# A two-layer streaming encoder: the modulation tiles of the time mixing start in the fourth period in place of the third

## The chip, the cores and the metric

The kernel runs on one core of one Trainium2 chip, in one launch. The metric is the device time of that launch in microseconds (us), a median over several runs. The core has five engines with a queue each: TensorE (PE, matmuls, with its weight loads PEld), VectorE (DVE), ScalarE (ACT), GpSimd (POOL) and SyncE (SP), which here issues nearly all DMAs.

## The reference

Two layers on 256 tokens of width 2048, 32 heads of 64. Layer 0 is RWKV-7 time mixing and an MLP with squared ReLU (hidden width 8192); layer 1 is a chunked band attention and such an MLP. Each sub-layer's input is normed, shifted and scaled, and its output gated, by vectors computed from a conditioning vector c:

```
mod = c @ w_ada[layer] + b_ada[layer]            # 2048 -> 6 * 2048, in each layer
sh1, sc1, gt1, sh2, sc2, gt2 = jnp.split(mod, 6, axis=-1)
...
h = modulate(rms_norm(x, g_mix[layer]), sh1, sc1)
...
x = x + gt1[:, None, :] * y                       # y: time mixing or attention
h = modulate(rms_norm(x, g_mlp[layer]), sh2, sc2)
x = x + gt2[:, None, :] * sq_relu_mlp(h, w_up[layer], w_down[layer])
```

The shared keys and values of layer 1 have a shift and a scale of their own (w_ada_kv). The time mixing is, per head, a recurrence over tokens; everything is float32.

## The kernel before

**Matmuls.** Weights come as float32 tiles of 128 x 1024 (512 KB, tag `raw`, 6 buffers), two for a block of 128 output columns. `halves` (L371 to L382) splits each into a rounded part `wH` (ACT, L378) and a remainder `wL` (DVE, L381), with 3 buffers each; the activations are split in the same way. `proj2` (L406 to L414) then multiplies a block: per 128 inputs one matmul of `wH` with both parts of the activations (L412) and one of `wL` with the larger part (L413), into a PSUM bank `pj`.

**Modulation.** c is a vector, so c @ w_ada isn't given to PE (but for the first shift and scale, which stand ahead of the time mixing). It is cut into 384 tiles of 128 x 1024 (`ada_tiles`, L427): 12 vectors, two halves each, 16 tiles to a half. `ada_load` (L434) issues a tile's DMA on SP. `ada_step` (L443) takes one tile: one DVE instruction that scales it with its 128 entries of c and adds it to `acc` (L452 for the first of a half, L454 for the others). `acc` has one buffer. When a half has its 16 tiles, `ada_sum` (L471 to L481) adds over the partitions with 32 small matmuls (L476) and one DVE instruction (L480) that writes the vector's half; the next half's first tile waits for the sum. The order of the vectors is fixed: (0, 2), (0, 4), (0, 3), (0, 5), then ("kv", 1), ("kv", 0), and those of layer 1. The pair is the layer and the index in mod above, counted from 0.

Who takes tiles, and how many: `self.ada(n)` takes n. In the time mixing a tile's DMA is issued at the place where it is taken and uses the `raw` buffers. Later, inside `ada_room(n)`, tiles have n buffers of their own (`rada`), and `ada_fill` keeps n - 1 of them loaded ahead. `ada_need(keys)` takes tiles until the named vectors are complete, all at that place.

**The time mixing** (`layer_a`, L630 to L900). The 32 heads are 16 pairs. For each pair the projections k and r are computed (`proj_steps`, 32 steps of one 128-input piece, each two matmuls), and then `Pair.steps`, 36 steps: 8 early ones, 12 that invert a triangular matrix, 16 late ones with the state. An invert step is a short chain through engines: a DVE transpose (`tt`, L239), small matmuls (`iv`, L111), a copy on ACT (L243), matmuls again, an addition on DVE (L254). The slots are a schedule by hand: a loop over 164 slots, 8 to a period (`S = self.SLOTS`), where pair j projects in period j (counted from 0) and makes its 36 steps in the 36 slots after that. So the first period has projections alone, the second adds the early steps of pair 0, the third its first 8 invert steps and pair 1's early steps, and from the sixth on four to five pairs are in work. In each slot every live pair makes one step, then 4 pieces of the projection follow (after slot 127 pieces of the output projection w_o), and then, in three slots of four, one modulation tile is taken.

The order on each engine isn't quite the order in the program: the compiler framework that builds the queues places instructions by their place in the program and by the time at which it expects their inputs and buffers. An instruction can so stand in its engine's queue ahead of others that come earlier in the program, and each queue is then executed in order.

**After the time mixing** `run` demands (0, 2), (0, 4) and (0, 3), 96 tiles, ahead of the output projection. The first MLP (`mlp`, L944 to L1012) has five `rada` buffers. Hidden columns go in four quarters of 16 blocks, each with 16 blocks up and 16 blocks down. `ada_tick` takes 1 and 2 tiles in turn after each block, in the first quarter from the seventh block up on. When the first quarter's 16 blocks up are through, one line demands the gate that the down blocks apply to x (L998):

```
if q == 0:
    self.ada_need((layer, 5))
```

Of the kernel before, what the change touches and what calls it, by code (L numbers as in the profile page):

```python
# [329 lines left out]
class Body:  # L330
# [299 lines left out]
    def layer_a(self, st, sp):  # L630
# [184 lines left out]
        with ExitStack() as s1:  # L815
# [12 lines left out]
            def proj_steps(pr):  # L828
                for dst, hl in (("k", xk), ("r", xr)):
                    w = self.wnext  # L830
                    src = next(weights, None)
                    self.wnext = None if src is None else self.weight(src)
                    ps = pp.tile([P, 2, T], F32, tag="pj", bufs=2, name="pj")
                    for kt in range(KT):
                        self.proj2(ps, w, lambda kt: hl[:, kt, :, 0:T], (kt, kt + 1))
                        if dst == "r" and kt == 1:
                            pr.lw = pw.tile([96, 2, P], F32, tag="lw", bufs=1, name="lw")
                            nc.sync.dma_start(out=pr.lw, in_=d["lora2"][pr.j, :96, 0:2])
                        if kt % 2 == 1:
                            if kt == KT - 1:  # L840
                                t = pw.tile([P, T], F32, tag=dst, bufs=2, name=dst)
                                nc.scalar.copy(t, ps[:, 0, :])
                                nc.vector.tensor_tensor(out=t, in0=ps[:, 1, :], in1=t, op=ALU.add)
                                setattr(pr, dst, t)
                            yield

            def out_steps():

                for n in range(8):
                    self.split(self.y_hl, n, v[:, n, :])  # L850
                sums, todo = self.o_ps, [(n, 0, HK) for n in range(8)] + [(n, HK, KT - 2) for n in range(4)]
                for n, lo, hi in todo:
                    if n % 2 == 0 and lo == 0:
                        tag = ("pj", "pj", "gr", "iv")[n // 2]
                        ps = pp.tile([P, 2 * T], F32, tag=tag, bufs=1 + (tag == "pj"), name="o")
                        sums.append(ps.rearrange("p (i t) -> p i t", i=2))
                    if lo == HK and n == 0:
                        assert all(p.done for p in pairs[:KT - 2])
                        for j in range(HK, KT - 2):
                            self.split(self.y_hl, j, v[:, j, :])  # L860
                    w = self.weight_part(d["w_o"][n], lo, hi)
                    for kt in range(lo, hi, 2):
                        self.proj(sums[n // 2][:, n % 2, :], w, lambda kt: self.y_hl[:, kt, :, 0:T],
                                  (kt, kt + 2), n % 2 == 0, False)
                        yield

            self.o_ps = []
            S, OUTS = self.SLOTS, 44
            inverts = range(Pair.EARLY, Pair.EARLY + Pair.INVERT)
            outs, done, n_out = None, 0, 0  # L870
            for slot in range(S * NPAIR + Pair.STEPS):
                live = []
                for j, pr in enumerate(pairs):
                    at = slot - S * (j + 1)
                    if 0 <= at < Pair.STEPS:
                        if at == 0:
                            pr.gen = pr.steps()
                        live.append((0 if at in inverts else 1 + (at < Pair.EARLY), -at, pr))
                        pr.done = at == Pair.STEPS - 1
                last = self.last_pe()  # L880
                for _, _, pr in sorted(live, key=lambda x: x[:2]):
                    with tc.issue_after(last):
                        next(pr.gen)
                    last = self.last_pe()
                if slot < S * NPAIR:
                    if slot % S == 0:
                        dense = proj_steps(pairs[slot // S])
                    todo = 16 // S
                else:
                    if outs is None:  # L890
                        self.y_hl = self.new_hl()
                        outs = dense = out_steps()
                    todo = OUTS * (slot + 1 - S * NPAIR) // Pair.STEPS - n_out
                    n_out += todo
                with tc.issue_after(last):
                    for _ in range(todo):
                        next(dense, None)
                if slot >= 2 * S and slot % 4 < 3:
                    self.ada()
            self.fin(HK)  # L900
        return v
# [305 lines left out]
```

## Time and profile before

| | |
|---|---|
| median of 3 runs | 2673.67 us (2671.55 to 2675.52) |
| profiled execution, its own time | 2673.81 us |
| its span | 2672.0 us, 1.8 us less than its time |
| granted TensorE clock, mean | 0.994 |
| DMA | 662.64 MB, mean 248 GB/s |
| tiles taken in the time mixing | 111 (first load at 223.8 us, last at 700.2 us) |
| tiles with `rada` buffers | 273 |

Times in the views are us from the start of the span. A group's row gives line, engine, operation, tiles written and read, shape and count. "L111" is line 111 of the kernel. "<-" after an idle time names what ended it. The granted clock is a share of full speed. The time mixing's first projection matmul starts at 209.0 us, the first output block that has all its inputs at 735.5 us, the first MLP runs from 786.5 us, the attention from 1518.2 us and the second MLP from 1938.9 us.

### The profile page before, as it was taken

How to read it: one execution, taken by the hardware profiler on the slowest of the kernel's cores; microseconds unless marked ns; L12 is line 12 of the kernel's file. 1: busy time of each engine (PE TensorE's matmuls, PEld its weight loads, DVE VectorE, ACT ScalarE, POOL GpSimd, SP SyncE). 2: the span in 40 equal slices, each digit the busy share in tenths (PEclk: the TensorE clock that was granted, in tenths of full speed). 3: DMA queues.
4: the chain of work that ended last, by engine and by line, in shares of the span. 5: the costliest groups of instructions: out<-in, count | busy, mean ns of one | idle time of the engine just before them, and what ended most of it. 6: DMA issues, size and time to landing. Idle time of an engine off the chain costs nothing. (4 is left out here: it accounts for less than half of the span.)

```text
span 2672.0 us, 58365 instructions
## 1 busy us (share of the span) xinstructions
PE 2600.1 (97%) x23690; PEld 2225.4 (83%) x23690; DVE 2101.0 (79%) x3109; ACT 1343.9 (50%) x2432; POOL 209.7 (8%) x320
## 2 busy tenths in 40 slices
PE   6999999999999999999999999999999999999997
PEld 3777788788899888888888998877898888888886
DVE  5778888889789888888888898899887556555555
ACT  3345555555456445355365554565564463453554
POOL 0001322332110000000000100000100000000002
PEclk9999999999999999999999999999999999999999
DMA  9966556565768888899898679887766555555553
GB/s 337 314 236 211 192 173 210 189 206 195 245 240 304 324 309 321 322 324 331 320 328 294 238 240 325 324 274 259 264 216 237 186 187 188 189 186 185 189 189 119
DMA packets 217390, 662.64 MB, mean 248 GB/s; under 512 B 21408, under 2 KB 68896, under 8 KB 217120
## 3 DMA queue, kind: packets, MB, share of 16 engines
q1 hardware_dynamic: 215056, 656.36, 71.1%
q8 instruction: 186, 3.05, 0.5%
q10 hardware_dynamic: 2064, 2.54, 0.3%
q14 instruction: 84, 0.69, 0.1%
HBM read 656.72 MB, written 2.10 MB: 247 GB/s over the span
## 5 line engine op out<-in xcount | busy, mean ns | idle before, releaser
L381 DVE TENSOR_TENSOR wL<-raw,wH 128x1024 fp32r<-128x1024 f32 x772 | 940.9, 1220 | 342.6 <-ACT wH L378 337.8
L378 ACT CAST wH<-raw 128x1024 fp32r<-128x1024 f32 x772 | 805.5, 1045 | 801.2 <-PE pj L412 646.0
L412 PE MATMUL pj<-aHL,wH 128*128 128x512 f32 x3328 | 1201.9, 403 | 2.0 <-DVE x L927 1.1
L413 PE MATMUL pj<-aHL,wL 128*128 128x256 f32 x3328 | 936.3, 281 | 0.0
L412 PEld LDWEIGHTS pj<-aHL,wH 128*128 128x128 f32 x3328 | 629.5, 189 | 154.1 <-issue 9.2
L412 PE MATMUL pj<-hHL,wH 128*128 128x512 f32 x2048 | 724.6, 399 | 0.0
L413 PEld LDWEIGHTS pj<-aHL,wL 128*128 128x128 f32 x3328 | 629.7, 189 | 2.6 <-issue 0.8
L413 PE MATMUL pj<-hHL,wL 128*128 128x256 f32 x2048 | 574.7, 281 | 0.0
L412 PEld LDWEIGHTS pj<-hHL,wH 128*128 128x128 f32 x2048 | 384.8, 188 | 95.7 <-DVE hHL L973 0.2
L413 PEld LDWEIGHTS pj<-hHL,wL 128*128 128x128 f32 x2048 | 387.0, 189 | 0.1
L454 DVE SCALAR_TENSOR_TENSOR acc<-rada,ct,acc 128x1024 f32<-128x1024 f32 x256 | 327.5, 1279 | 8.4 <-DMA rada<-w_ada 7.5
L518 POOL TENSOR_TENSOR ss<-ss,sq 128x256 f32<-128x256 f32 x56 | 54.5, 974 | 1590.8 <-ACT sq L517 1590.5
L998 DVE SCALAR_TENSOR_TENSOR x<-pj,mod,x 128x256 f32<-128x256 f32 x256 | 123.3, 482 | 59.5 <-PE pj L413 55.7
L454 DVE SCALAR_TENSOR_TENSOR acc<-raw,ct,acc 128x1024 f32<-128x1024 f32 x104 | 136.4, 1312 | 15.5 <-DMA raw<-w_ada 15.4
L401 PE MATMUL pj<-aHL,wH 128*128 128x258 f32 x384 | 109.0, 284 | 0.0
L402 PE MATMUL pj<-aHL,wH 128*128 128x258 f32 x384 | 109.0, 284 | 0.0
L970 ACT ACTIVATE t<-t 128x256 f32<-128x256 f32 x112 | 46.8, 418 | 122.6 <-DVE t L942 122.6
L403 PE MATMUL pj<-aHL,wL 128*128 128x258 f32 x384 | 108.0, 281 | 0.0
L403 PEld LDWEIGHTS pj<-aHL,wL 128*128 128x128 f32 x384 | 73.2, 191 | 0.2
L402 PEld LDWEIGHTS pj<-aHL,wH 128*128 128x128 f32 x384 | 72.6, 189 | 0.1
L401 PEld LDWEIGHTS pj<-aHL,wH 128*128 128x128 f32 x384 | 72.2, 188 | 0.2
L972 ACT ACTIVATE t<-t 128x256 f32<-128x256 f32 x128 | 53.4, 417 | 3.4
(244 smaller groups left out, 2812.3 us busy)
## 6 DMA issues: line engine op xcount, KB each, us to landing
raw<-w_up SPq DMA_DIRECT2D x256, 512.0 KB, 4.1
raw<-w_down SPq DMA_DIRECT2D x256, 512.0 KB, 4.1
rada<-w_ada SPq DMA_DIRECT2D x209, 512.0 KB, 5.7
raw<-w_ada SPq DMA_DIRECT2D x111, 512.0 KB, 4.4
rawa<-w_ada SPq DMA_DIRECT2D x64, 512.0 KB, 6.8
rada<-w_ada_kv SPq DMA_DIRECT2D x64, 512.0 KB, 6.6
raw<-w_k SPq DMA_DIRECT2D x32, 512.0 KB, 4.2
raw<-w_r SPq DMA_DIRECT2D x32, 512.0 KB, 4.5
```

The costliest lines, as they stand in the source:

```text
L378: nc.scalar.copy(Hf, raw)
L381: eng.tensor_tensor(out=Lf, in0=raw, in1=Hf, op=ALU.subtract)
L401: nc.tensor.matmul(ps, H[:, i, :], a(kt)[:, 0, :], start=(first and kt == 0), stop=False)
L402: nc.tensor.matmul(ps, H[:, i, :], a(kt)[:, 1, :], start=False, stop=False)
L403: ins = nc.tensor.matmul(ps, L[:, i, :], a(kt)[:, 0, :], start=False, stop=(last and kt == KT - 1))
L412: nc.tensor.matmul(ps, H[:, i, :], a(kt), start=(kt == 0), stop=False)
L413: ins = nc.tensor.matmul(ps[:, 0, :], L[:, i, :], a(kt)[:, 0, :], start=False, stop=(kt == KT - 1))
L454: nc.vector.scalar_tensor_tensor(out=self.acc, in0=raw, scalar=ck, in1=self.acc, op0=ALU.mult, op1=ALU.add)
L518: (eng or nc.gpsimd).tensor_tensor(out=self.ss, in0=self.ss, in1=sq, op=ALU.add)
L970: nc.scalar.activation(t, t, AF.Relu)
L972: nc.scalar.activation(t, t, AF.Square)
L998: nc.vector.scalar_tensor_tensor(out=x, in0=ps[:, i, :], scalar=self.mods[(layer, 5)][:, n:n + 1], in1=x, op0=ALU.mult, op1=ALU.add)
```

## The change

The condition in the slot loop of `layer_a` under which a tile is taken has its bound raised by one period of eight slots:

```diff
                 with tc.issue_after(last):
                     for _ in range(todo):
                         next(dense, None)
-                if slot >= 2 * S and slot % 4 < 3:
+                if slot >= 3 * S and slot % 4 < 3:
                     self.ada()
             self.fin(HK)
         return v
```

Slots 16 to 23 take no tile any more. The tiles' order is the same and none is dropped: each slot from 24 on takes the tile that the slot eight before it took. `ada`, `ada_tick` and `ada_need` are unchanged, and the number of tiles that the later calls take follows from what was taken before.

## The prediction

> **What bounds the kernel now.** I read the page's head first, then busy time by stretches, then what TensorE waited for, in order of time.
>
> ```profile
> span 2672.0 us, 58365 instructions
> ...
> PE 2600.1 (97%) x23690; PEld 2225.4 (83%) x23690; DVE 2101.0 (79%) x3109; ACT 1343.9 (50%) x2432; POOL 209.7 (8%) x320
> ```
>
> TensorE (PE) is busy for 97% of the span, so a change can gain only where PE stands still or runs at a lower clock. The next view gives busy time in three stretches of the time mixing. The columns are the stretch, its length, busy time of PE, PEld, DVE, ACT and POOL, the granted clock (1.00 is full), DMA share and GB/s. The first two stretches are the third and the fourth period of eight slots, cut at the first matmul of k of pairs 2, 3 and 4. The last runs from k of pair 5 to r of pair 15, which is 10.5 periods.
>
> ```profile
> 237.80:263.40 25.60, 22.53 (x377) 18.09 (x376) 22.45 (x37) 12.32 (x30) 6.07 (x7) 0.93 0.67 217
> 263.40:294.30 30.90, 26.16 (x479) 21.55 (x477) 24.96 (x44) 13.49 (x36) 8.80 (x11) 0.89 0.64 202
> 322.30:621.30 299.00, 293.82 (x6126) 240.43 (x6124) 258.35 (x493) 162.69 (x458) 87.57 (x119) 1.00 0.59 192
> ```
>
> In the long run PE is busy 98% and a period takes 299.0/10.5 = 28.5 us. The third period has fewer pairs, yet PE stands still for 3.1 us in it; the fourth takes 30.9 us, with 4.7 us of standstill. Both ran below full clock. The timeline of PE tells where (start, duration, then in brackets the idle time before it and what ended it).
>
> ```profile
> 233.99 0.70 PE L115 MATMUL ms<-s,csts 128*128 128x256 f32 x2 [1.58 <-DVE s L174]
> ...
> 244.36 0.45 PE L111 MATMUL iv<-tt,al 32*32 32x32 f32 x32 [2.11 <-DVE tt L239]
> ...
> 256.23 0.46 PE L111 MATMUL iv<-tt,al 32*32 32x32 f32 x32 [0.96 <-DVE tt L239]
> ...
> 283.38 0.65 PE L111 MATMUL iv<-tt,al 32*32 32x32 f32 x32 [4.16 <-DVE tt L239]
> ```
>
> Each of these four waits ends with an instruction of VectorE (DVE). The clock falls behind the two long ones (same columns as above):
>
> ```profile
> 244.00:252.00 8.00, 7.64 (x122) 6.18 (x122) 5.67 (x12) 3.75 (x11) 1.57 (x3) 0.79 0.79 254
> 246.00:248.00 2.00, 2.00 (x18) 1.37 (x21) 1.81 (x3) 0.15 (x1) 0.00 (x0) 0.50 0.78 211
> 284.00:292.00 8.00, 8.00 (x97) 6.54 (x97) 4.22 (x7) 0.91 (x4) 0.00 (x0) 0.64 0.52 166
> ```
>
> After the 2.11 us of idleness PE gets half the clock for a while (0.50), and 0.79 over 8 us: 8 x 0.21 = 1.7 us lost. After the 4.16 us it is 8 x 0.36 = 2.9 us.
>
> **The change, part by part.** A modulation tile is one load of 512 KB and one DVE instruction. The loop takes a tile in three of four slots. Slots 16 to 163 are 148, three quarters of them 111, as the second row below says. From slot 24 on there are 140, so 105 tiles. Six tiles leave the third period and every later tile of the time mixing moves by exactly one period, at the same place within it. So do the sums of a finished half (16 tiles, L476 on PE, L480 on DVE).
>
> ```profile
> L454 DVE SCALAR_TENSOR_TENSOR acc<-rada,ct,acc 128x1024 f32<-128x1024 f32 x256 | 327.5, 1279 | 8.4 <-DMA rada<-w_ada 7.5
> ...
> raw<-w_ada SPq DMA_DIRECT2D x111, 512.0 KB, 4.4
> ```
>
> No tile disappears: the six (6 x 1.28 = 7.7 us of DVE, 3 MB on SP's queue) come later. Where? The first MLP takes 1.5 tiles per block of 128 hidden columns from its seventh on, 15 by the end of the first sixteen. Then everything up to the gate (0, 5), 128 tiles, is demanded at once. Before, 111 + 15 = 126 were done and the demand was 2; now 105 + 15 = 120 and the demand is 8. From there on the two programs take the same tiles at the same places.
>
> *What is removed.* DVE around the waits, from its timeline (L452 and L454 are the tiles):
>
> ```profile
> 227.57 0.97 DVE L452 TENSOR_SCALAR acc<-raw,ct 128x1024 f32<-128x1024 f32 x1
> 228.46 1.21 DVE L381 TENSOR_TENSOR wL<-raw,wH 128x1024 fp32r<-128x1024 f32 x1
> ...
> 233.86 1.63 DVE L454 SCALAR_TENSOR_TENSOR acc<-raw,ct,acc 128x1024 f32<-128x1024 f32 x1
> 235.41 0.41 DVE L185 TENSOR_TENSOR v<-ms,v 128x256 f32<-128x256 f32 x1
> ...
> 242.72 1.27 DVE L454 SCALAR_TENSOR_TENSOR acc<-raw,ct,acc 128x1024 f32<-128x1024 f32 x1
> 243.91 0.30 DVE L239 STREAM_TRANSPOSE tt<-u 128x128 f32<-128x128 f32 x1
> ```
>
> - Wait of 1.58 us at 233.99: tile 0 stands in the queue ahead of what PE waits for and takes 228.46 - 227.57 = 0.89 us of it. Without it the wait is 0.7 us: **-0.9** (bounds 0 and -1.58).
> - Wait of 2.11 us at 244.36: the fifth tile stands right before the transpose that PE waits for, 243.91 - 242.72 = 1.19 us; the second (235.41 - 233.86 = 1.55 us) and two more stand further up. 1.19 + 1.55 is more than 2.11, so I take the whole wait away: **-2.1** (bounds -1.2 and -2.1). With it the 1.7 us of low clock go: **-1.7** (bounds 0 and -1.7). What is late next is PE itself.
> - Wait of 0.96 us at 256.23: no tile stands directly before it, only DVE's general lateness. Half: **-0.5** (bounds 0 and -0.96).
> - Fourth period: it keeps six tiles, but no backlog enters from the third, where DVE was busy 22.45 of 25.60 us and now has some 8 us less to do. Bounds: 0, and the wait with its low clock, 4.16 + 2.9 = 7.1 us. The nearest row is the long run, where a period with six tiles and more pairs takes 28.5 us; I take 30.9 - 28.5: **-2.4**.
> - SP's queue: six loads fewer in the third period, where weights were not what was waited for: 0.
>
> Sum of the gains: -7.6 us.
>
> [...]
>
> *What is added.* DVE around the end of the first sixteen blocks of the MLP, and busy time in three stretches (the last is the second layer's MLP):
>
> ```profile
> 822.19 0.16 DVE L480 TENSOR_TENSOR mod<-m,bada 128x8 f32<-128x8 f32 x1
> ...
> 858.55 2.60 DVE L454 SCALAR_TENSOR_TENSOR acc<-rada,ct,acc 128x1024 f32<-128x1024 f32 x2
> ...
> 879.89 0.48 DVE L998 SCALAR_TENSOR_TENSOR x<-pj,mod,x 128x256 f32<-128x256 f32 x1
> ```
>
> ```profile
> 724.00:786.00 62.00, 62.00 (x390) 56.29 (x389) 52.00 (x62) 33.25 (x50) 12.97 (x14) 0.98 0.78 273
> 822.00:862.00 40.00, 40.00 (x250) 35.72 (x244) 39.70 (x46) 22.95 (x39) 0.00 (x0) 1.00 0.94 340
> 1986.00:2028.00 42.00, 42.00 (x300) 36.57 (x300) 41.51 (x48) 25.18 (x45) 0.00 (x0) 1.00 0.90 321
> ```
>
> DVE has 10 us free from 724 to 786 us, and the tiles that finish a half (now 105 to 111 in place of 111 alone) need no sum before they start: six more fit there (7.7 us). The sum that ends this half came at 822.19 in the seventh block; it now belongs to the eleventh, four blocks of about 5.65 us later, near 845. The next sixteen tiles took from 822 to 861 us, 39 us with DVE full; now they end near 884. The first x update (L998, 879.89) waits for them and is some 5 us late. PE has three banks for these results and so may go on for two more blocks, 11 us: 0.
>
> What is left is VectorE's half of a weight (wL, L381). The casts follow each other at PE's pace:
>
> ```profile
> 884.94 1.05 ACT L378 CAST wH<-raw 128x1024 fp32r<-128x1024 f32 x1 [1.78 <-PE pj L412]
> 887.77 1.05 ACT L378 CAST wH<-raw 128x1024 fp32r<-128x1024 f32 x1 [1.77 <-PE pj L412]
> ...
> 861.40 2.50 DVE L381 TENSOR_TENSOR wL<-raw,wH 128x1024 fp32r<-128x1024 f32 x2
> ```
>
> A cast starts when PE frees a buffer, two halves (2 x 2.83 = 5.66 us) before PE needs that buffer filled; cast and wL take 1.05 + 1.25, so DVE may be 3.4 us late. Two tiles in a row (2.60 us, 858.55) cost nothing; a third would. In the second MLP the same demand is 5 tiles (379 of 384 done by the same count), DVE is 41.51 of 42.00 us busy and PE never stops. For 8 tiles I take one tile's length: **+1.3** (bounds 0, and all eight in a row ahead of a wL, 8 x 1.28 - 3.4 = 6.8).
>
> Sum: -7.6 + 1.3 = -6.3 us. The profiled execution took 2673.81 us (1.8 us around its span), so 2667.5; the median of the three runs, 2673.67, is 0.1 us from it, and I leave the number. About 0.2% (5.3 us) is what a measurement of this kernel can tell from no change: below 2668.3 is faster, above 2679.0 slower.
>
> **The rivals.**
>
> A. *The wait moves.* Tile 0 ran at 227.57, ten microseconds before its period: tiles are placed ahead where DVE is thought free. If the first tiles of slot 24 come into the third period, or the fourth keeps its 4.16 us because it has its own six tiles, only -0.9 - 1.2 with no clock regained stays, less the 1.3: 2673.0; with the clock, 2671. For it: the 4.16 us wait stands in a period that keeps its load. Against: six fewer on an engine 88% busy.
>
> B. *The demand of eight stops PE* (the other side). The eight tiles stand in the program ahead of the first down weights. If they run in one piece, wL is 6.8 us late, and PE then gets the low clock as it did behind 4.16 us, 2.9 us more: +9.7. It decides from the third tile in a row on. With only 0.9 + 1.2 us gained: 2681.4. For it: DMA at 0.94 and DVE at 39.70 of 40.00 us in that stretch leave nothing to catch up with. Against: the five of the second MLP.
>
> C. *Nothing happens*: DVE's lateness in the third period is not what holds PE, since other work is behind it: 2672 to 2675. Against: the releaser of all four waits is DVE.
>
> **How the numbers follow.** Forecast 0.50, own range 2660 to 2671, with 0.43 of it below 2668.3; A 0.22, of which 0.02 falls below; B 0.20, of which 0.17 lies above 2679.0; C 0.08, of which 0.02 lies above. So faster 0.45, same 0.36, slower 0.19. All gains at their bounds without a cost would be 2673.8 - 13.4 = 2660; up to B's point of decision it is 2680. I give 2660 to 2680.
>
> **What would show it.** Right: no tile before about 245 us; PE's waits at 234 and 244 gone or under 1 us; clock 1.00 in the third period, which then takes 20 to 23 us; the fourth near 28.5; 105 loads raw<-w_ada; the sum at 822 moved to about 845; PE unbroken from 786 to 940. Wrong: a wait of over 2 us for tt still in the fourth period (A), PE waiting for wL between 865 and 900 us (B), or a third period of 25 us without tiles in it (C).

## The result, and the profile after

The median of the changed kernel is 2678.64 us (16 runs, 2674.74 to 2684.49), that of the kernel before on the same chip 2674.07 us (16 runs, 2668.79 to 2675.80). The ratio is 1.0022 with a 95% interval of 1.0015 to 1.0029: slower by 0.2%, where 2667.5 us was forecast. The profiled execution took 2677.74 us. Its page begins

```profile
span 2676.0 us, 58394 instructions
...
PE 2599.7 (97%) x23690; PEld 2223.2 (83%) x23690; DVE 2096.7 (78%) x3109; ACT 1344.4 (50%) x2432; POOL 212.8 (8%) x320
...
raw<-w_ada SPq DMA_DIRECT2D x105, 512.0 KB, 4.3
```

PE's work is the same (2599.7 us against 2600.1) and the span is 4.0 us longer: 4.4 us of standstill came in. The 105 loads are the 105 tiles that were counted. Where the 4.0 us arose is seen when the starts of weight blocks are compared, each taken from the first projection matmul. The table gives each kernel's lead (negative) or lag against the kernel before, in us; the last four columns belong to experiments told below.

| start of | before, at | after | spread | demand alone | queue part | later and spread |
|---|---|---|---|---|---|---|
| third period | 237.8 | 0.0 | 0.0 | 0.0 | 0.0 | -0.1 |
| fourth period | 263.4 | +0.5 | +1.4 | -0.2 | +0.5 | -3.2 |
| fifth period | 294.3 | -5.7 | -4.9 | -1.5 | -5.7 | -9.3 |
| r of pair 13 | 564.5 | -7.3 | -7.6 | -2.0 | -6.5 | -7.9 |
| k of pair 14 | 578.1 | -2.8 | -7.0 | -1.4 | -4.6 | -8.0 |
| first MLP | 786.5 | -3.0 | -3.8 | -0.6 | -0.9 | +0.4 |
| its first down block | 879.2 | -3.9 | -3.8 | -1.6 | -1.8 | +1.1 |
| fifth down block | 901.8 | +4.2 | -3.7 | +8.0 | 0.0 | +1.1 |
| last block | 2651.2 | +3.2 | -7.4 | +6.0 | -5.1 | -2.2 |

So the time mixing did gain, and 8.1 us went within four blocks behind the demand of the gate. (4.5 us between r of pair 13 and k of pair 14 belong to this one execution, as the second run of the changed kernel shows below.) First the gain. These are the two periods of the changed kernel, cut at the same matmuls as before (stretch, length, busy PE, PEld, DVE, ACT, POOL, clock, DMA share, GB/s), and two short stretches of the first:

```profile
238.60:264.70 26.10, 22.61 (x377) 18.23 (x376) 21.21 (x36) 12.32 (x30) 6.78 (x7) 0.93 0.55 174
264.70:289.40 24.70, 23.31 (x478) 19.25 (x477) 20.47 (x40) 13.69 (x36) 7.17 (x11) 1.00 0.59 189
256.00:258.00 2.00, 1.98 (x50) 1.75 (x50) 1.20 (x1) 0.64 (x2) 1.67 (x2) 0.62 0.80 250
258.00:260.00 2.00, 2.00 (x8) 1.63 (x6) 1.11 (x1) 0.00 (x0) 0.00 (x0) 0.53 0.82 236
```

The third period, from which the tiles were to go, takes 26.1 us (25.6 before) at the same clock of 0.93. The fourth, which keeps six tiles in the program, takes 24.7 us (30.9 before) at full clock. PE's timeline of the changed kernel has the waits:

```profile
234.79 0.70 PE L115 MATMUL ms<-s,csts 128*128 128x256 f32 x2 [1.54 <-DVE s L174]
...
243.42 0.45 PE L111 MATMUL iv<-tt,al 32*32 32x32 f32 x32 [0.36 <-DVE tt L239]
...
256.02 0.45 PE L111 MATMUL iv<-tt,al 32*32 32x32 f32 x32 [3.13 <-DVE tt L239]
...
275.87 0.45 PE L111 MATMUL iv<-tt,al 32*32 32x32 f32 x32 [1.39 <-DVE tt L239]
```

The waits were 1.58, 2.11, 0.96 and 4.16 us. The first didn't move (1.54). The second shrank to 0.36, and the third took its place with 3.13, low clock included (0.62 and 0.53). The fourth is gone: the same matmuls now start at 281.26 us without a wait, at full clock. The 1.39 us stand before an earlier invert step, which waited less in the kernel before:

```profile
273.77 0.45 PE L111 MATMUL iv<-tt,al 32*32 32x32 f32 x32 [0.58 <-DVE tt L239]
```

DVE's timeline says why the third grew:

```profile
243.19 0.71 DVE L452 TENSOR_SCALAR acc<-raw,ct 128x1024 f32<-128x1024 f32 x1
...
247.95 1.49 DVE L454 SCALAR_TENSOR_TENSOR acc<-raw,ct,acc 128x1024 f32<-128x1024 f32 x1
...
252.24 0.27 DVE L254 TENSOR_TENSOR u<-u,iv 128x128 f32<-128x128 f32 x1
...
254.10 1.21 DVE L381 TENSOR_TENSOR wL<-raw,wH 128x1024 fp32r<-128x1024 f32 x1
255.24 0.41 DVE L175 TENSOR_TENSOR kh<-s 128x256 f32<-128x256 f32 x1
255.57 0.30 DVE L239 STREAM_TRANSPOSE tt<-u 128x128 f32<-128x128 f32 x1
255.80 1.40 DVE L454 SCALAR_TENSOR_TENSOR acc<-raw,ct,acc 128x1024 f32<-128x1024 f32 x1
```

L452 at 243.19 is the first tile of slot 24, whose period begins at 264.7. Five of the six tiles of the fourth period were placed ahead, into the third (243.19, 247.95, 255.80, 258.89 and 261.82 us). The kernel before places tiles ahead in the same way: three of the third period's own six ran in the second, and three of the fourth's ran in the third. So the third period went from six tiles to five, and DVE's work in it from 22.45 to 21.21 us. The tile at 247.95 stands in front of the addition (252.24) and the transpose (255.57) that PE waits for, and 3.1 us of other work, a weight's half among it, came between those two.

Now the loss. PE, behind the demand (the longest of its waits):

```profile
896.56 0.39 PE L413 MATMUL pj<-hHL,wL 128*128 128x256 f32 x1 [2.38 <-DVE wL L381]
...
901.00 0.39 PE L413 MATMUL pj<-hHL,wL 128*128 128x256 f32 x1 [0.76 <-DVE wL L381]
```

The releaser named is DVE. One must go on to what released DVE: wL needs the cast wH, and the casts on ACT waited for the weights' transfer.

```profile
888.70 1.05 ACT L378 CAST wH<-raw 128x1024 fp32r<-128x1024 f32 x1 [6.85 <-DMA raw<-w_down]
892.57 1.05 ACT L378 CAST wH<-raw 128x1024 fp32r<-128x1024 f32 x1 [2.83 <-DMA raw<-w_down]
898.65 1.05 ACT L378 CAST wH<-raw 128x1024 fp32r<-128x1024 f32 x1 [5.02 <-DMA raw<-w_down]
```

And the transfers were late because they were issued late. SP's timeline (start and length of a group of issues, the waits within it included):

```profile
874.05 0.38 SPq L368 DMA_DIRECT2D raw<-w_down  x1
876.29 5.50 SPq L368 DMA_DIRECT2D rada<-w_ada_kv  x4
881.88 0.38 SPq L368 DMA_DIRECT2D raw<-w_down  x1
883.79 1.91 SPq L368 DMA_DIRECT2D rada<-w_ada_kv  x2
885.79 0.47 SPq L368 DMA_DIRECT2D raw<-w_down  x1
888.09 4.46 SPq L368 DMA_DIRECT2D rada<-w_ada_kv  x2
892.61 0.90 SPq L368 DMA_DIRECT2D raw<-w_down  x2
```

By the program the demand uses up the four tiles that are loaded ahead, loads the other four itself, and leaves it to the first tick behind it to load four ahead again. Each of these loads goes into the buffer of an earlier tile and can't start before DVE has worked that buffer off (from 860 to 905 us SP waited for L454 12 times, 19.0 us in all, up to 3.7). Four of them stand in SP's queue ahead of one weight load and hold it for 5.5 us; two more hold the one after the next for 4.46 us. In the 18.6 us from 874.05 to 892.61 three weight loads were issued, one in 6.2 us, where PE takes a tile of 128 x 1024 in 2.83 us. In the kernel before, with two tiles demanded, more weights went out early, and between later ones stands one tile load or two:

```profile
861.60 5.64 SPq L368 DMA_DIRECT2D raw<-w_down  x4
874.45 0.33 SPq L368 DMA_DIRECT2D rada<-w_ada_kv  x1
874.87 0.97 SPq L368 DMA_DIRECT2D raw<-w_down  x1
...
880.42 0.38 SPq L368 DMA_DIRECT2D raw<-w_down  x1
883.22 2.76 SPq L368 DMA_DIRECT2D rada<-w_ada_kv  x2
886.07 0.38 SPq L368 DMA_DIRECT2D raw<-w_down  x1
```

The one at 886.07 is the tenth weight load of the down blocks, the second of the fifth block. In the changed kernel the tenth is one of the two from 892.61 on.

### The profile page after: what moved, and what is told of

Its sections match the earlier page's. It is cut to its first block, busy times and chain, and to the rows that moved or that the text cites. A ratio compares the mean times of both kernels' runs of the same rounds, so it can differ in the third digit from the quotient of the medians.

```text
span 2676.0 us, 58394 instructions
## 1 busy us (share of the span) xinstructions
PE 2599.7 (97%) x23690; PEld 2223.2 (83%) x23690; DVE 2096.7 (78%) x3109; ACT 1344.4 (50%) x2432; POOL 212.8 (8%) x320
## 4 chain that ended last, share of the span: by engine, by line
PE 79%; DVE 7%; DMA 3%; issue 3%; ACT 2%; POOL 0%; DVEq 0%; SPq 0%; ACTq 0%; POOLq 0%
PE pj L412 43%; PE pj L413 21%; DVE wL L381 2%; PE pj L402 2%; PE pj L401 2%; PE pj L403 2%; DVE acc L454 1%; PE iv L111 1%; DMA raw<-w_ada 1%; ACT wH L378 1%; PE gr L105 1%; DMA raw<-w_down 1%; DMA rada<-w_ada 1%; PE ms L115 1%; PE ms L105 1%
## 5 line engine op out<-in xcount | busy, mean ns | idle before, releaser
L454 DVE SCALAR_TENSOR_TENSOR acc<-rada,ct,acc 128x1024 f32<-128x1024 f32 x262 | 335.0, 1278 | 11.4 <-DMA rada<-w_ada 10.6
L454 DVE SCALAR_TENSOR_TENSOR acc<-raw,ct,acc 128x1024 f32<-128x1024 f32 x98 | 128.0, 1306 | 17.3 <-DMA raw<-w_ada 16.9
L970 ACT ACTIVATE t<-t 128x256 f32<-128x256 f32 x112 | 46.8, 418 | 110.2 <-DVE t L942 110.2
L941 ACT COPY t<-pj 128x256 f32<-128x256 f32 x112 | 41.2, 368 | 39.4 <-PE pj L413 39.2
```

What stands on the lines that cost most here:

```text
L454: nc.vector.scalar_tensor_tensor(out=self.acc, in0=raw, scalar=ck, in1=self.acc, op0=ALU.mult, op1=ALU.add)
L970: nc.scalar.activation(t, t, AF.Relu)
```

## The experiments

All kernels compute everything that the kernel before computes; only places and queues differ. Each was timed in five rounds beside the kernel before, whose medians were 2672.64 us (first four), 2673.27 (next four) and 2672.35 us (last two). I went in with the theory that the time mixing gains and the demand loses by SP's queue; rivals were that the loss belongs to where the tiles stand in general, or that the gain isn't one.

**The demand made small, the change kept** ("spread" in the table). The ticks of the first MLP begin four blocks earlier, 21 tiles in place of 15, so that 105 + 21 = 126 are done at the gate and the demand is 2, as before.

```diff
-            if q or f >= RAW - 2:
+            if q or f >= (2 if layer == 0 else RAW - 2):
                 self.ada_tick(layer)
```

> The changed kernel, with the first MLP taking its tiles from the third block on in place of the seventh: 6 tiles more by the end of the sixteen blocks up, so the demand at that place is 2 again and not 8. The time mixing is that of the changed kernel. Theory 1 (the time mixing gained about 3 us up to the first MLP, the demand of eight then lost 8 us): the loss between 876 and 907 us goes, total 2669 to 2672, that is 2 to 5 us below the kernel before. Rival (the loss is not of the demand but of the tiles' shift through the whole MLP): total stays at 2677 to 2680.

Measured: 2666.57 us, ratio 0.9979 (0.9969 to 0.9990). By the ratios this beats both kernels, by 0.2% and 0.4%, and is a little better than expected. The stretch of the loss, in this kernel (columns as above):

```profile
876.00:902.00 26.00, 26.00 (x149) 22.51 (x148) 25.89 (x28) 9.48 (x9) 0.00 (x0) 1.00 0.94 334
```

PE has no standstill, though the DMA share is 0.94 and DVE is busy for 25.89 of 26.00 us. In the changed kernel it is

```profile
876.00:902.00 26.00, 20.58 (x169) 16.22 (x168) 23.52 (x27) 6.30 (x6) 0.00 (x0) 1.00 0.94 316
```

with 5.4 us of standstill: the same DMA share and less work on DVE. Neither DVE's load nor the DMA share explains the loss.

**The demand alone.** The kernel before, with the ticks four blocks later: 111 + 9 = 120 tiles at the gate, a demand of 8.

```diff
-            if q or f >= RAW - 2:
+            if q or f >= (RAW + 2 if layer == 0 else RAW - 2):
```

> The kernel before, with the first MLP taking its tiles only from the eleventh block on in place of the seventh: the time mixing is untouched, the demand at the end of the blocks up is 8 in place of 2. Theory 1 (the demand of eight is the loss): PE stands still between 876 and 910 us, total 2680 to 2684, some 8 us above the kernel before. Rival (the loss comes from the time mixing): 2672 to 2676.

Measured: 2679.33 us, ratio 1.0029 (1.0018 to 1.0041), just under the expectation. The lead of -1.6 us at the first down block becomes a lag of 8.0 at the fifth (the table). The loss of the change is so made without its edit, by the demand alone. (In this execution it includes 3.4 us at half clock, from 895.6 us on.)

**All tile loads from the MLP's buffers on GpSimd's queue,** the change kept.

```diff
-        self.nc.sync.dma_start(out=t, in_=src)
+        (self.nc.gpsimd if ada and self.ada_pool else self.nc.sync).dma_start(out=t, in_=src)
```

> The changed kernel, with the tiles that have buffers of their own (rada) loaded from GpSimd's queue in place of SyncE's; the demand stays 8. Theory 1a (the weights are late because their loads stand in SyncE's queue behind tile loads that wait for VectorE to free a buffer): the casts no longer wait for weights, the 8 us go, total 2669 to 2673. Theory 1b (the weights are late because the transfers' total rate is used up): the casts wait for weights as before, total 2677 to 2681. Theory 1c (VectorE works off the tiles ahead of the weights' halves): PE waits for wL with the weights long landed, 2677 to 2681.

Measured: 2690.62 us, ratio 1.0077 (1.0064 to 1.0091). As a whole a miss. At the demand the expectation holds: from -1.9 us at the first down block to +0.1 at the fifth, 2.0 us lost in place of 8.1. But the lag goes from 3.9 us at 1622 to 18.2 at 1782, in the attention, where PE waited for

```profile
PE m L1060 <- DVE vf L942: 5.5, 6, 1.8
PE pT L1102 <- DVE s L1091: 3.2, 1, 3.2
PE S L1080 <- DVE q L942: 2.0, 1, 2.0
```

(us in total, times, longest). Why DVE is late there with the loads on another queue was not followed further.

**The fifth period.** The bound raised once more: 99 + 15 = 114 tiles at the gate, a demand of 14.

```diff
-                if slot >= 3 * S and slot % 4 < 3:
+                if slot >= 4 * S and slot % 4 < 3:
```

> The bound raised by one period more (slot 32): 99 tiles in the time mixing, the demand is 14. Theory 1 (each tile that the demand takes over what was loaded costs PE its transfer and its DVE time): 6 tiles more at 1.3 us, so 7 to 9 us above the changed kernel, 2685 to 2690, less what the fourth period gains without tiles (0 to 4 us). Rival (the loss is a fixed price of a late sum): within 2 us of the changed kernel.

Measured: 2692.92 us, ratio 1.0076 (1.0064 to 1.0089), slower than expected. From -3.1 us at the first down block the lag grows to 12.0 at the sixth and 18.2 by 1512 us: the loss grows with the demand. ACT, from 860 to 925 us, and the third and fourth period of this kernel:

```profile
ACT wH L378 <- DMA raw<-w_down: 21.3, 4, 8.2
```

```profile
238.10:260.90 22.80, 21.47 (x379) 17.30 (x379) 15.96 (x33) 12.22 (x30) 5.38 (x7) 1.00 0.28 99
260.90:288.20 27.30, 24.47 (x477) 20.11 (x476) 19.80 (x38) 13.73 (x36) 6.18 (x11) 0.94 0.49 152
```

Here no tile runs in the third period, and it takes 22.8 us at full clock; the long wait has moved on into the fourth (2.30 us at 272.88).

**A part of the loads on GpSimd's queue** ("queue part"). To leave the attention alone, only the tiles that stand around the demand go there. The demand stays at 8.

```diff
+            self.pool_queue = (key, half) in (((0, 5), 1), (("kv", 1), 0), (("kv", 1), 1))
...
-        self.nc.sync.dma_start(out=t, in_=src)
+        (self.nc.gpsimd if ada and self.pool_queue else self.nc.sync).dma_start(out=t, in_=src)
```

> The changed kernel, with only 48 tiles (the second half of the gate (0, 5) and the vector (kv, 1), those around the demand) loaded from GpSimd's queue; all others stay on SyncE's. Theory 1a (weights' loads stand behind tile loads in SyncE's queue): PE loses at most 2 us between 876 and 910 us instead of 8, and the losses that the run with all rada loads on GpSimd's queue had in the output projection and the attention do not come: total 2669 to 2673. Rival 1b (transfer rate used up): 2677 to 2681.

Measured: 2673.84 us, ratio 1.0000 (0.9991 to 1.0008), just above the expectation. The demand loses 1.8 us (-1.8 to 0.0) in place of 8.1. SP's timeline in this kernel has weights alone, and ACT's waits from 860 to 905 us name no transfer any more:

```profile
857.31 54.29 SPq L368 DMA_DIRECT2D raw<-w_down  x20
```

```profile
ACT wH L378 <- PE pj L412: 19.7, 12, 3.5
```

The same eight tiles are taken at the same place. So it is their loads on SP's queue, ahead of weights, that cost some 6 of the 8 us; 1.8 remain for everything else. (No run leaves the loads on SP and changes their order alone.) What this kernel gains there it loses in part ahead of the MLP: -3.5 us at the first output block become -0.9 at 786.

**The early ticks without the change.** Meant as a control of the first experiment: its edit, in the kernel before. That makes 132 tiles by the gate, no demand, and every later tile four places early.

> The kernel before, with the first MLP taking tiles from its third block on: no tile is left to demand (132 of 128), the time mixing is untouched. Theory 1 (a demand of 2 cost nothing, so the 6 us of the spread version come from the time mixing): 2671 to 2675, within 2 us of the kernel before. Rival (the spread itself is what gained): 2665 to 2669.

Measured: 2684.53 us, ratio 1.0042 (1.0028 to 1.0055): a miss. It is no clean control. 5 us go between 786 and 879 (not followed), and 8.8 between 1512 and 1564, where PE waits for the last addition of a norm's sum of squares on DVE:

```profile
1527.22 1.19 PE L523 MATMUL m<-ss,csts 128*128 128x256 f32 x2 [4.78 <-DVE ss L518]
```

**The second period.** The bound lowered by one period from the original: 117 + 15 = 132 tiles at the gate, no demand.

```diff
-                if slot >= 3 * S and slot % 4 < 3:
+                if slot >= S and slot % 4 < 3:
```

> The bound lowered by one period (slot 8): 117 tiles in the time mixing, none left to demand. Theory 1: six tiles more on VectorE in the second period, where it was busy 15.3 of 17.5 us, so PE waits there 3 to 7 us longer, with nothing to gain at the demand (2 cost nothing): 2675 to 2681. Rival (only the number of tiles at the demand counts): within 2 us of the kernel before.

Measured: 2689.83 us, ratio 1.0063 (1.0051 to 1.0075), a miss in size. The direction in the time mixing is as expected (a lag of 7.9 us at the fourth period), but 6.4 of it are back at the fifth. The rest is lost later, at the norms: 5.8 us ahead of the MLP, and 8.4 between 1512 and 1564, as in the experiment before this one, with which it shares the 132 tiles at the gate.

```profile
237.38 1.22 PE L115 MATMUL ms<-s,csts 128*128 128x256 f32 x2 [3.87 <-DVE s L174]
...
790.22 1.22 PE L523 MATMUL m<-ss,csts 128*128 128x256 f32 x2 [3.85 <-DVE ss L518]
```

**The changed kernel again,** unchanged, for what is its own and what one execution's.

> The changed kernel as it is, on the chip of these runs and with a second profile. Expected: 4 to 6 us above the kernel before; loss of 8 us between 876 and 907 us again; the wait of 1.95 us at 569.85 us that no instruction ended ('issue'), with its low clock, not again (2.8 us less lost there), since the two kernels that share this part of the program did not have it in their profiles.

Measured: 2676.75 us, ratio 1.0012 (1.0004 to 1.0021); 1.0015 to 1.0021 lies in both intervals. The 3.13 us wait in the third period and the loss at the demand (-6.2 to +1.7) are there again. The half clock behind that wait is not: the third period takes 24.7 us at 1.00 here, and 26.1 at 0.93 in the first execution (the last section has what the traces show of it). The 4.5 us that the table shows between r of pair 13 and k of pair 14 are not (1.1 here): they belong to one execution.

**A clean control of the early ticks.** The kernel before, without tiles in the last eight slots of the time mixing in place of slots 16 to 23, and with the early ticks: 105 + 21 = 126, a demand of 2.

```diff
-                if slot >= 2 * S and slot % 4 < 3:
+                if 2 * S <= slot < S * NPAIR + Pair.STEPS - 8 and slot % 4 < 3:
```

> The time mixing of the kernel before, but with no tile in its last eight slots (105 tiles, as many as the changed kernel), and the first MLP taking tiles from its third block on: 126 before the demand, which is 2, and from there on the same tiles at the same places as in the kernel before and in the spread version of the changed kernel. Theory 1 (the spread version's 6 us come from the third and fourth period): no gain there, 2671 to 2675, at most 2 us below the kernel before. Rival (the spread in the MLP is what gains): 2666 to 2669.

Measured: 2671.06 us, ratio 0.9993 (0.9985 to 1.0002), as expected. With the count at the gate kept at 126, the early ticks give nothing that can be measured. The two kernels differ only in which eight slots go without tiles, the third period's or the last ones: by the ratios 0.9993 - 0.9979 = 0.14%, 3.7 us, are the gain of the later begin. The two intervals overlap a little (0.9985 to 1.0002 and 0.9969 to 0.9990), so that a gain is likely but its size is loose.

**Half a period later, with ticks from the first block** ("later and spread"). 102 + 24 = 126, a demand of 2.

```diff
-                if slot >= 3 * S and slot % 4 < 3:
+                if slot >= 3 * S + 4 and slot % 4 < 3:
...
-            if q or f >= RAW - 2:
+            if layer == 0 or q or f >= RAW - 2:
```

> Tiles from slot 28 on (102 in the time mixing) and in the first MLP from its first block on: 126 before the demand, which is 2. Theory 2 (tiles of the fourth period that are placed ahead into the third keep PE waiting there): the third period takes 22.5 to 23.5 us in place of 26 and the total is 2 to 3 us below the spread version, 2663 to 2666. Rival (tiles among the first two blocks of the MLP hold up the norm that PE waits for there): PE waits 2 to 5 us between 780 and 800 us, total 2666 to 2671.

Measured: 2674.32 us, ratio 1.0008 (0.9999 to 1.0016), above what any theory expected. In the time mixing it did what it was made for (third and fourth period):

```profile
238.00:260.60 22.60, 21.27 (x382) 17.02 (x376) 17.76 (x33) 12.59 (x32) 5.38 (x7) 1.00 0.38 123
260.60:285.00 24.40, 22.89 (x471) 18.87 (x471) 20.86 (x39) 13.43 (x35) 7.13 (x11) 1.00 0.58 189
```

With the first tile at 255.6 us both are short and at full clock, and the lead is 9.3 us. It is gone at the norm ahead of the MLP, where a tile stands on DVE in front of the sum of squares and waits for its own transfer (DVE's timeline, then PE's, then the clock behind it):

```profile
782.43 1.28 DVE L454 SCALAR_TENSOR_TENSOR acc<-rada,ct,acc 128x1024 f32<-128x1024 f32 x1 [1.47 <-DMA rada<-w_ada]
...
784.03 0.42 DVE L518 TENSOR_TENSOR ss<-ss,sq 128x256 f32<-128x256 f32 x1
```

```profile
784.50 1.22 PE L523 MATMUL m<-ss,csts 128*128 128x256 f32 x2 [4.00 <-DVE ss L518]
```

```profile
785.00:789.00 4.00, 4.00 (x19) 3.82 (x19) 3.02 (x4) 1.14 (x3) 0.00 (x0) 0.50 0.63 228
```

From the block at 780.4 to the one at 786.5 of the kernel before, a lead of 5.6 us becomes a lag of 0.4. The 4.00 us and half of the 4 us at 0.50 make these 6.0. The tile in front accounts for 1.47 + 1.2 = 2.7 of the 4.00; the rest was not followed.

## Why the prediction was wrong, step by step

**The failed step is the price of the demand: "For 8 tiles I take one tile's length: +1.3".** It cost 8.1 us in the profile, 7.8 by the demand alone (0.29% of 2672.64). I asked how late DVE may be with wL, and bounded the answer at 6.8 by eight tiles in a row on DVE. The 1.8 us that remain with the loads on another queue are near the 1.3; that they are this lateness is not shown. What I left out are the loads that the eight tiles issue, in the queue that also brings PE's weights. The stretch of the second MLP that I leaned on couldn't show it: by the program's order almost no tile is left to load behind its demand (384 in all, 379 done, up to four loaded ahead). That this is why it was free was read from the program and not tried.

The other steps:

- *Six tiles leave the third period and every later tile keeps its place within a period:* that holds in the program, not on DVE. In the order in which DVE ran them, the second period lost three tiles, the third one (six to five) and the fourth two (seven to five). So the "some 8 us less" of DVE work in the third period were 1.2, and the gains below are wrongly divided.
- *Wait of 1.58 us at 233.99, -0.9:* nothing; 1.54 us is left. Tile 0 stood in front but wasn't what the wait was made of.
- *Wait of 2.11 us at 244.36 and its clock, -2.1 and -1.7:* it shrank by 1.75 us, and the half clock behind it went. But in the first execution both came back at 256, with 3.13 us at 0.53 to 0.62; in the second only the wait did.
- *Wait of 0.96 us at 256.23, -0.5:* it grew to 3.13. With no tile in front of it (half a period later, and in the fifth period) it is 0.96 us as before, and the third period takes 22.6 and 22.8 us at full clock. So the 20 to 23 us that I named as a sign were to be had, and the tiles placed ahead took them: in this period rival A happened, by the mechanism that it gave.
- *Fourth period, 30.9 to 28.5, -2.4:* 24.7, so -6.2. The long run's 28.5 us per period was the wrong row, since its periods hold four to five pairs. The upper bound, 7.1, was nearer.
- *Sum of the gains, -7.6:* 7.3 us in the profile by 564 us, 3.9 of them left at the demand; 8.9 and 6.2 in the second execution, where the lead shrinks from 8.3 to 5.7 us between 628 and 735 (not followed); 3.7 us by the ratios of the two kernels that differ only in where the six tiles are missing. Right in sign and, early on, in size, and wrongly divided.
- *Six tiles fit between 724 and 786 us, 0:* right; the lead is -3.3 at 735.5 and -3.0 at 786.5. *The sum moves from 822 to 845:* it came at 842.53. *The x update 5 us late, 0:* it ran at 876.29, ahead of the sum at 880.61, and waited for nothing.
- *Rival B, +9.7:* right in place and sign, and near in the 6.8 us of its wait, with a chance of 0.20. Its mechanism, eight tiles in one piece on DVE, isn't what happened, and the 2.9 us of low clock didn't come in the changed kernel (1.00 from 876 to 902). With the demand alone some came (0.93 over 876 to 902).

The parts close: 3.7 us gained and 7.8 lost make +4.1 us; the two comparisons of the changed kernel give 5.9 (0.22%) and 3.2 (0.12%). The 7.8 alone has an interval of 4.8 to 11.0 us, so no smaller term can be told from this.

On the clock: it stayed at 1.00 behind the 2.38 us at 896.56 of the changed kernel, and was 0.53 behind its 3.13 us (first execution, 258 to 260 us) and 0.50 behind the 2.11 us of the kernel before; with the 4.00 us of "later and spread" it is at 0.50 from 783.14 us on, 2.6 us into them. So the length of a wait alone doesn't tell what follows it here. The last section has what the traces show.

## What to carry to other kernels

When work is moved that issues DMAs, price it on the queue that issues them: here four tile loads that waited for buffers held the weight load behind them for 5.5 us, and two more held another for 4.46 us; a demand of eight tiles cost 8 us, some 6 of them that way, and a demand of two nothing. When a wait names an engine, follow what released that engine, too; two steps on (DVE, ACT, SP) stood another cause. And in this kernel, with PE 97% busy, a gain won early was kept only where the later meeting points, the gate and the norms, saw the same backlog as before (between the first and the fifth down block the lead went from -3.9 us to +4.2 in the changed kernel and from -3.8 to -3.7 in the spread version): the best version was the one that moved the tiles and kept the demand at two.

## What the runs showed of the hardware that was not expected

- Waits that together held PE for 5.4 of 26 us left its clock at 1.00 (876 to 902), while behind one of 2.11 us it fell to 0.50, and so it did behind one of 3.13 us in one execution of the changed kernel (0.50 from 256.48 to 259.90 us) and not in the next (1.00). In the traces of the kernel before and of the changed kernel all changes of the granted clock within a trace lie whole multiples of 3.41 us apart (from 209 to 2650 us: at 245.44, 248.86, 282.99, 289.82, 723.31 and 726.72 us in the first, at 256.48, 259.90, 570.51, 573.92, 679.74 and 683.15 us in the second), at places that differ between the two, so PE's busy time can be read between two such places. Below are the kernel before, with 0.50 in the next such stretch; the changed kernel again, two stretches, with 1.00 behind them; and the changed kernel at the wait of 2.38 us, with 1.00 behind it:

```profile
242.03:245.44 3.41, 1.30 (x37) 1.02 (x36) 2.83 (x4) 2.47 (x6) 0.62 (x1) 1.00 0.73 249
251.85:255.26 3.41, 1.68 (x10) 1.21 (x8) 3.41 (x8) 1.04 (x1) 0.69 (x1) 1.00 0.66 232
255.27:258.67 3.40, 2.01 (x53) 1.83 (x54) 2.57 (x4) 0.64 (x2) 3.04 (x2) 1.00 0.50 155
894.82:898.23 3.41, 1.67 (x10) 1.50 (x11) 3.37 (x4) 0.00 (x0) 0.00 (x0) 1.00 0.94 278
```

  PE stood still for 2.11, 1.73, 1.39 and 1.74 us of them. The 3.13 us wait was cut in two by such a place, and so was the one of 2.38 us; in the first execution, where 2.9 of the 3.13 us fell into one stretch, the next 3.41 us ran at half clock. With the demand alone two waits fell into one stretch (892.20 to 895.60, PE busy for 1.10 us), and 0.50 followed. Between 209 and 2650 us the two traces have six stretches with full clock in them and half clock behind them; PE stood still in them, summed, for 2.11, 3.41 and 2.77 us (the kernel before) and for 2.95, 1.95 and 1.38 us (the changed kernel). The longest standstills with full clock behind them are 1.58 and 1.74 us. So the sum within one stretch told what followed in all of these but the 1.38 us (676.30 to 679.70), and a fixed limit isn't shown. The same wait of 3.13 us was followed by 3.41 us at half clock in one execution (by this 1.7 us lost) and by none in the other.
- A block of 16 matmul pairs mostly took 5.61 to 5.66 us (232 blocks of the kernel before, 196 of the changed kernel), but 5.55 in 3 blocks of the first and 35 of the second, in a stretch of up to 14 blocks (78 us) at the same clock of 1.00; from 1251 to 1301 us, for one. The places differ between the two, and by these numbers a stretch of 14 gives 0.8 to 1.4 us. What makes them was not found; that some of the leads at the last block in the table come from it is an estimate.
- The same loads on GpSimd's queue were good for the demand (2.0 us lost in place of 8.1) and bad for the attention (14 us lost).
